# Two gated products in a seven-product block form: a decoder trunk on one Trainium2 core

## The chip, the cores and the metric

The kernel runs on one core of one Trainium2 chip, as one program. The metric is the device time of one execution in microseconds (us), the median over runs. Engines are named as in the profile: PE (TensorE matmul) and PEld (its weight load), DVE (VectorE), ACT (ScalarE), POOL (GpSimd), SP (SyncE, which issues the transfers here).

## The reference, cut to what matters

A trunk of two layers over 528 tokens (16 learned ones and 512 real ones) with 1024 channels: a state-space layer with a GLU, a feed-forward net, an attention layer, a second feed-forward net, a last norm. The feed-forward net is what the change touches:

```python
def rmsnorm(x, gain):
    x32 = x.astype(jnp.float32)
    y = x32 * lax.rsqrt(jnp.mean(x32 * x32, axis=-1, keepdims=True) + RMS_EPS)
    return (y * gain.astype(jnp.float32)).astype(x.dtype)

def swiglu_ffn(h, w_in, w_out):
    gu = jnp.einsum('bld,df->blf', h, w_in)
    g, u = jnp.split(gu, 2, axis=-1)
    return jnp.einsum('blf,fd->bld', jax.nn.silu(g) * u, w_out)

h = h + swiglu_ffn(rmsnorm(h, norm_ffn[i]), w_ffn_in[i], w_ffn_out[i])
```

D_MODEL is 1024 and D_FF 2816, all in float32. "Both gated products" are the einsum with `w_in`, gate and up, of both layers.

## The kernel before

Channels lie on the 128 partitions, tokens along the free axis: `h[k]` is k-tile k (of KD = 8) with 528 columns, 512 from the attention on. Every weight matrix is cut into tiles of 128 output channels. A matmul with float32 accuracy is made from three terms: weight and operand are each split into a high part of type fp32r and the rest, w = wh + wl and x = xh + xl, and wh xh, wh xl and wl xh are summed in PSUM.

The order of everything is written out by hand: each engine executes its instructions in the order in which the program issues them. The weights are one list, `steps`, of up to 8 k-tiles (128x1024) each. `w_load` issues their transfers on SP into three buffers, two steps ahead; `w_split` (from L102) makes wh on ACT (L113) and wl = raw - wh on DVE (L114); `w_next` splits AHEAD = 2 steps ahead and gives a step to the matmuls; `mm_steps` (from L124, matmul at L135) runs the k-tiles and the three terms over one or two column blocks.

`ffn` serves both feed-forward nets. For each of KF = 22 blocks f of hidden channels it makes the gate (`pg`) and the up product (`pu`): in layer 0 in two column blocks of 264 each, 2 x 8 x 3 x 2 = 96 matmuls, in layer 1 in one block of 512 columns (`pgu`), 48 matmuls. Then DVE scales the gate by `rstd` (L809), ACT makes Silu (L810), POOL multiplies it by `rstd` (L811), DVE multiplies by the up product (L812), ACT makes `hh` (L813) and DVE `hl` (L814). After all 22 blocks the projection out (`po`) runs over d = 0 to 7 with 22 k-tiles each in three steps (8, 8 and 6 k-tiles), adds to `h[d]` (L826, L828), and sums squares on POOL (`ssq_add`, L162 to L166). `split_x` (L156, L157) makes the xh and xl of the next stage. `tail` is the last d of layer 1 with the final norm, in two halves of 256 columns (L1180).

PSUM in `ffn` is four tiles of two banks each. The hidden tiles `hh` and `hl` of all 22 blocks lie in SBUF at once.

Of the kernel before, what the change touches and what calls it, by code (L numbers as in the profile page):

```python
# [30 lines left out]
AHEAD = 2  # L31
SQB = 6
# [11 lines left out]
OFF = {0: 0, 1: 128, 2: 256, 3: 384}  # L44


@with_exitstack
def trunk_kernel(ctx, tc, xu, xn, prm, octp, gvec, c_id, c_rev, c_i16, c_blk, c_mask,
# [19 lines left out]

    def add_w(src, n, kt):
        for f in range(n):  # L70
            k0 = 0
            while k0 < kt:
                nk = min(8, kt - k0)
                steps.append((src, f, k0, nk))
                k0 += nk

    for f in range(N1F):
        steps.append((w_glu, f, 0, GLU1[f]))
    for f in (2 * p_ + j for p_ in PAIRS for j in ((0, 1) if p_ != PAIRS[-1] else (1, 0))):
# [12 lines left out]

    def w_load(n):
        while state["load"] <= min(n, len(steps) - 1):
            i = state["load"]
            src, f, k0, nk = steps[i]
            r = raw_p.tile([128, 8, 128], F32, tag="raw", name=f"raw{i}")
            sp.dma_start(out=r[:, 0:nk, :], in_=src[f, :, k0 * 128:(k0 + nk) * 128].rearrange("p (k m) -> p k m", m=128))
            raws[i] = r
            state["load"] += 1  # L100

    def w_split(n):  # L102
        while state["split"] <= min(n, len(steps) - 1):
            i = state["split"]
            w_load(i + 2)
            src, f, k0, nk = steps[i]
            r = raws.pop(i)[:, 0:nk, :]
            if alt:
                wh, wl = alt.pop(0)()
            else:  # L110
                wh = wh_p.tile([128, 8, 128], F32R, tag="wh", name=f"wh{i}")
                wl = wl_p.tile([128, 8, 128], F32R, tag="wl", name=f"wl{i}")
            act.activation(out=wh[:, 0:nk, :], in_=r, func=ACTF.Copy)  # L113
            dve.tensor_tensor(out=wl[:, 0:nk, :], in0=r, in1=wh[:, 0:nk, :], op=ALU.subtract)  # L114
            splits[i] = (wh, wl)
            state["split"] += 1

    def w_next(ahead=AHEAD):
# [3 lines left out]
        return splits.pop(i), steps[i][3], steps[i][2]  # L122
# [35 lines left out]

    def ssq_add(k, ssq, n, first):
# [1167 lines left out]
```

## Time and profile before

| | us |
|---|---|
| median of 3 runs | 1281.71 (1281.14 to 1282.2) |
| profiled execution, its own time | 1283.81 |
| its span, first to last instruction | 1282.0 |
| PE busy | 1207.2 (94%) |
| DVE busy | 707.8 (55%) |
| ACT busy | 484.6 (38%) |
| POOL busy | 326.4 (25%) |
| gate/up products of layer 0 | about 233 to 489 |
| projection out of layer 0 | about 489 to 617 |
| gate/up products of layer 1 | about 898 to 1145 |
| projection out of layer 1 | about 1145 to 1270 |

A busy time is the sum of what the profile shows for an engine's instructions; where an instruction waits for a port inside its own run, the wait is part of it. Matmuls are pipelined, so what one costs is read from start to start, not from its own duration. The stages are told apart by the tiles that the matmuls write (`pg`, `pu`, `pgu`, `po`).

### The profile page before, as it was taken

How to read it: one execution, taken by the hardware profiler on the slowest of the kernel's cores; microseconds unless marked ns; L12 is line 12 of the kernel's file. 1: busy time of each engine (PE TensorE's matmuls, PEld its weight loads, DVE VectorE, ACT ScalarE, POOL GpSimd, SP SyncE). 2: the span in 40 equal slices, each digit the busy share in tenths (PEclk: the TensorE clock that was granted, in tenths of full speed). 3: DMA queues.
4: the chain of work that ended last, by engine and by line, in shares of the span. 5: the costliest groups of instructions: out<-in, count | busy, mean ns of one | idle time of the engine just before them, and what ended most of it. 6: DMA issues, size and time to landing. Idle time of an engine off the chain costs nothing.

```text
span 1282.0 us, 19763 instructions
## 1 busy us (share of the span) xinstructions
PE 1207.2 (94%) x8206; PEld 1100.9 (86%) x8206; DVE 707.8 (55%) x987; ACT 484.6 (38%) x738; POOL 326.4 (25%) x290
## 2 busy tenths in 40 slices
PE   3588899999999999999989999989999999999996
PEld 3578899999999999999979999868788888888886
DVE  8899547643433343433678888985644444442224
ACT  5544343432223222222557666753332323321120
POOL 6444027210110110111144444444311101111110
PEclk8689899999999999999999999999999999999998
DMA  3455523232233323333212221122233333223321
GB/s 98 88 110 114 106 77 110 77 117 86 83 100 86 94 81 91 91 91 95 87 50 57 62 64 50 50 66 80 69 99 99 99 99 94 88 88 96 102 74 66
DMA packets 44919, 110.15 MB, mean 86 GB/s; under 512 B 4766, under 2 KB 17950, under 8 KB 44830
## 3 DMA queue, kind: packets, MB, share of 16 engines
q1 hardware_dynamic: 43024, 107.64, 29.5%
q8 instruction: 64, 1.05, 0.3%
q10 hardware_dynamic: 1805, 1.26, 0.3%
q14 instruction: 26, 0.20, 0.1%
HBM read 106.14 MB, written 2.74 MB: 85 GB/s over the span
## 4 chain that ended last, share of the span: by engine, by line
PE 73%; DVE 6%; ACT 1%; issue 1%; POOL 0%; DVEq 0%; ACTq 0%; POOLq 0%
PE pgu L135 19%; PE po L135 18%; PE pu L135 10%; PE pg L135 10%; PE pj L135 7%; PE pj L1089 2%; DVE ga L985 2%; PE w L1027 1%; PE pv L1048 1%; PE po L1180 1%; DVE wl L114 1%; PE z L977 1%; PE z L1089 1%; PE z L976 1%; DVE xl L157 1%
## 5 line engine op out<-in xcount | busy, mean ns | idle before, releaser
L114 DVE TENSOR_TENSOR wl<-raw,wh 128x1024 fp32r<-128x1024 f32 (+5 forms) x194 | 242.8, 1257 | 223.8 <-ACT wh L113 220.4
L113 ACT ACTIVATE wh<-raw 128x1024 fp32r<-128x1024 f32 (+5 forms) x194 | 189.1, 979 | 242.4 <-PE po L135 120.2
L811 POOL TENSOR_TENSOR s<-s,rstd 128x528 f32<-128x528 f32 (+1 forms) x44 | 57.4, 1305 | 439.7 <-ACT s L810 439.7
L135 PE MATMUL pgu<-xl,wh 128*128 128x512 f32 x352 | 138.7, 394 | 1.0 <-DVE xl L157 1.0
L135 PE MATMUL pgu<-xh,wh 128*128 128x512 f32 x352 | 138.3, 393 | 0.6 <-ACT xh L156 0.6
L135 PE MATMUL pgu<-xh,wl 128*128 128x512 f32 x352 | 138.4, 393 | 0.0
L135 PE MATMUL po<-hh,wh 128*128 128x264 f32 (+1 forms) x506 | 132.0, 317 | 0.0
L135 PE MATMUL po<-hh,wl 128*128 128x264 f32 (+1 forms) x506 | 131.9, 317 | 0.0
L135 PE MATMUL po<-hl,wh 128*128 128x264 f32 (+1 forms) x506 | 131.8, 317 | 0.0
L135 PE MATMUL pg<-xh,wl 128*128 128x264 f32 x536 | 109.5, 286 | 2.3 <-DVE wl L114 2.3
L135 PE MATMUL pg<-xl,wh 128*128 128x264 f32 x536 | 109.6, 286 | 1.9 <-DVE xl L157 1.9
L135 PE MATMUL pg<-xh,wh 128*128 128x264 f32 x536 | 110.2, 287 | 1.2 <-ACT ysb L627 0.9
L998 POOL TENSOR_TENSOR be<-be,ga 128x415 f32<-128x415 f32 (+1 forms) x48 | 58.1, 1210 | 127.5 <-DVE ga L985 111.5
L135 PEld LDWEIGHTS po<-hh,wh 128*128 128x128 f32 x506 | 83.2, 188 | 7.2
L135 PEld LDWEIGHTS po<-hl,wh 128*128 128x128 f32 x506 | 83.3, 187 | 7.1
L135 PEld LDWEIGHTS po<-hh,wl 128*128 128x128 f32 x506 | 83.1, 188 | 7.1
L810 ACT ACTIVATE s<-g 128x528 f32<-128x528 f32 (+1 forms) x44 | 28.1, 638 | 153.9 <-DVE g L809 153.9
L135 PEld LDWEIGHTS pg<-xh,wl 128*128 128x128 f32 x536 | 83.3, 189 | 2.7 <-DVE wl L114 2.7
L135 PEld LDWEIGHTS pg<-xh,wh 128*128 128x128 f32 x536 | 83.5, 188 | 2.4 <-ACT ysb L627 1.6
L135 PEld LDWEIGHTS pg<-xl,wh 128*128 128x128 f32 x536 | 83.1, 188 | 2.6 <-DVE xl L157 2.6
L165 POOL TENSOR_TENSOR sq<-h 128x528 f32<-128x528 f32 (+1 forms) x27 | 36.8, 1363 | 173.2 <-DVE h L826 94.1
L135 PEld LDWEIGHTS pgu<-xl,wh 128*128 128x128 f32 x352 | 66.0, 188 | 17.0 <-DVE xl L157 1.7
(338 smaller groups left out, 2566.8 us busy)
## 6 DMA issues: line engine op xcount, KB each, us to landing
raw<-in_w_in SPq DMA_DIRECT2D x88, 512.0 KB, 3.5
raw<-in_w_out SPq DMA_DIRECT2D x32, 512.0 KB, 3.8
raw<-in_w_kv SPq DMA_DIRECT2D x16, 512.0 KB, 3.6
raw<-in_w_out SPq DMA_DIRECT2D x16, 384.0 KB, 3.2
m<-rd SPq DMA_DIRECT2D x8, 512.0 KB
raw<-in_w_q SPq DMA_DIRECT2D x8, 512.0 KB, 3.5
raw<-in_w_o SPq DMA_DIRECT2D x8, 512.0 KB, 3.4
op<-in_octp SPq DMA_DIRECT2D x8, 352.0 KB, 7.1
```

Of the source, the lines that this page charges most:

```text
L113: act.activation(out=wh[:, 0:nk, :], in_=r, func=ACTF.Copy)
L114: dve.tensor_tensor(out=wl[:, 0:nk, :], in0=r, in1=wh[:, 0:nk, :], op=ALU.subtract)
L135: pe.matmul(ps[pc][:, 0:n], lhsT=w[:, k, :], rhs=x[kk][:, c0:c0 + n], start=(first and k == 0 and j == 0), stop=(last and k == nk - 1 and ...
L157: dve.scalar_tensor_tensor(out=xl[k], in0=h[k][:, 0:n], scalar=g, in1=xh[k], op0=ALU.mult, op1=ALU.subtract)
L165: e.tensor_tensor(out=sq[:, 0:n], in0=h[k][:, 0:n], in1=h[k][:, 0:n], op=ALU.mult)
L810: act.activation(out=s_, in_=g_, func=ACTF.Silu)
L811: pool.tensor_tensor(out=s_, in0=s_, in1=rstd[:, 0:n], op=ALU.mult)
L976: pe.matmul(o_, lhsT=qhh[hd][:, q0:q0 + 128], rhs=khl[hd][:, k0:k0 + nn], start=True, stop=False)
L977: pe.matmul(o_, lhsT=ql[hd][:, q0:q0 + 128], rhs=khl[hd][:, k0:k0 + nn], start=False, stop=True)
L985: dve.tensor_tensor_scan(out=ga[:, c0:c1], data0=ga[:, c0:c1], data1=hide[:, m0:m0 + c1 - c0], initial=init, op0=ALU.mult, op1=ALU.max)
L998: pool.tensor_tensor(out=be[:, 1:n], in0=be[:, 1:n], in1=ga[:, 0:n - 1], op=ALU.mult)
L1089: pe.matmul(ps, lhsT=w[:, k, :], rhs=x[k], start=(k == 0 and j == 0), stop=(k == KD - 1 and j == 2))
```

## The change

The gate/up product of a block f becomes one 2 x 2 block product in seven multiplications in place of eight. The weights are cut into A11 (gate, k-tiles 0 to 3), A12 (gate, 4 to 7), A21 (up, 0 to 3), A22 (up, 4 to 7); the operand into B11, B12 (k-tiles 0 to 3, first and second half of the tokens), B21, B22 (k-tiles 4 to 7). Weight sums are S1 = A21 + A22, S2 = S1 - A11, S3 = A11 - A21, S4 = A12 - S2; operand sums T1 = B12 - B11, T2 = B22 - T1, T3 = B22 - B12, T4 from T2 and B21. Products are numbered P1 (A11 B11), P2 (A12 B21), P3 (S4 B22), P4 (A22 T4), P5 (S1 T1), P6 (S2 T2), P7 (S3 T3). Each is 4 k-tiles times three split terms over half the tokens (264 columns in layer 0, 256 in layer 1).

P1 and P2 share a PSUM bank, P5 and P3 another, P7 and P4 a third; the rest of the sums is made on DVE. The weight sums are made on POOL from the raw tiles, and each of the seven weight operands is split on ACT and DVE by itself. The hidden blocks run in three chunks (6, 8 and 8 blocks), each with its own projection out into `h`, so that `hh` and `hl` hold one chunk. `steps` now has two kinds of entries (d: direct, b: block); `b_next` splits up to BAHEAD = 4 products ahead, POOL's sums are issued up to five steps before that, and the raw tiles of odd blocks get buffers of their own. At the entry of each layer the seven operands are made from `h` (class `Combos`) in place of eight `split_x`; the squares of the last `h` tile go to the norm as a sum of their own. The lines that this takes from the diff, cut:

```diff
+BAHEAD = 4
+CHUNKS = ((0, 6), (6, 14), (14, 22))
+WHICH = {1: "A11", 2: "A12", 3: "S4", 4: "A22", 5: "S1", 6: "S2", 7: "S3"}
+XOF = {1: "B11", 2: "B21", 3: "B22", 4: "T4", 5: "T1", 6: "T2", 7: "T3"}
+def products(f0, f1):
+    out = []
+    for f in range(f0, f1):
+        if f == 0:
+            out += [(1, 0), (1, 1), (5, 0), (5, 1)]
+        elif f > 1:
+            out += [(1, f), (5, f)]
+        if f > f0:
+            out += [(3, f - 1), (4, f - 1)]
+        out += [(6, f), (2, f), (7, f)]
+    return out + [(3, f1 - 1), (4, f1 - 1)]
...
+    def make_sum(L, f, tag):
...
+        pool.tensor_tensor(out=t, in0=a, in1=b, op=op)
...
+    def sums_ahead(i, to):
+        for j in range(max(0, i - 4), min(i + to, len(steps) - 1) + 1):
+            if steps[j][0] == "b" and steps[j][2] == 5 and f"u{(steps[j][1], steps[j][3])}" in raws and steps[j][1] in scope:
+                all_sums(steps[j][1], steps[j][3])
...
+                _, L, m, f = steps[i]
+                loads_to(i, 11)
+                sums_ahead(i, 5)
+                r = block(L, m, f)
...
+                act.activation(out=wh, in_=r, func=ACTF.Copy)
+                dve.tensor_tensor(out=wl, in0=r, in1=wh, op=ALU.subtract)
...
+            def mm(p, ps, first, last):
+                wh, wl = b_next()
+                for k in range(4):
+                    xh, xl = cx.c[XOF[p], k]
+                    for j, (w, x) in enumerate(((wh, xh), (wh, xl), (wl, xh))):
+                        pe.matmul(ps[:, 0:m], lhsT=w[:, k], rhs=x, start=(first and k == 0 and j == 0),
+                                  stop=(k == 3 and j == 2), skip_group_check=True)
...
+            for c, (f0, f1) in enumerate(CHUNKS):
+                for q, (p, f) in enumerate(products(f0, f1)):
...
+                    mm(p, s[tag], p in (1, 5, 6, 7), True)
...
+                    if p == 1:
+                        s["m1"] = half_tile("m1")
+                        act.activation(out=s["m1"], in_=ps, func=ACTF.Copy)
+                    elif p == 6:
...
+                        add(s["u1"], ps, s["m1"])
+                        add(s["uu"][:, m:n], s["Z"][:, 0:m], s["u1"])
...
+                    elif p == 2:
+                        s["g"] = ft.tile([128, n], F32, tag="g", name="g")
+                        dve.tensor_tensor(out=s["g"][:, 0:m], in0=ps, in1=rstd[:, 0:m], op=ALU.mult)
+                    elif p == 7:
+                        add(s["uu"][:, m:n], ps, s["uu"][:, m:n])
+                    elif p == 3:
+                        g_ = s["g"]
+                        add(g_[:, m:n], ps, s["u1"])
+                        dve.tensor_tensor(out=g_[:, m:n], in0=g_[:, m:n], in1=rstd[:, m:n], op=ALU.mult)
+                        s["s"] = ft.tile([128, n], F32, tag="s", name="s")
+                        act.activation(out=s["s"], in_=g_, func=ACTF.Silu)
+                        pool.tensor_tensor(out=s["s"], in0=s["s"], in1=rstd[:, 0:n], op=ALU.mult)
+                    elif p == 4:
+                        add(s["uu"][:, 0:m], ps, s["u1"])
...
+                        dve.tensor_tensor(out=s["s"], in0=s["s"], in1=s["uu"], op=ALU.mult)
+                        act.activation(out=hh[i], in_=s["s"], func=ACTF.Copy)
+                        dve.tensor_tensor(out=hl[i], in0=s["s"], in1=hh[i], op=ALU.subtract)
...
+                for d in range(KD):
...
+                    for _ in mm_steps(ps, Off(hh, f0), Off(hl, f0), cols):
+                        pass
+                    for pc, c0, nn in cols:
+                        dve.tensor_tensor(out=h[d][:, c0:c0 + nn], in0=h[d][:, c0:c0 + nn], in1=ps[pc][:, 0:nn], op=ALU.add)
```

## Rows read from the trace of the kernel before

**Rows 1.** The page, part 1: busy us (share of the span), instructions

```profile
PE 1207.2 (94%) x8206; PEld 1100.9 (86%) x8206; DVE 707.8 (55%) x987; ACT 484.6 (38%) x738; POOL 326.4 (25%) x290
```

**Rows 2.** Busy time by stretch (gate/up of layer 0, of layer 1), columns named

```profile
core 0: us, PE busy (x) PEld busy (x) DVE busy (x) ACT busy (x) POOL busy (x), PEclk, DMA share, GB/s
255.00:488.00 233.00, 233.00 (x1906) 233.00 (x1905) 90.23 (x102) 66.61 (x81) 27.44 (x21) 1.00 0.32 94
...
913.00:1145.00 232.00, 232.00 (x1005) 188.32 (x1005) 97.64 (x111) 71.09 (x87) 27.03 (x21) 1.00 0.30 94
```

**Rows 3.** The chain that ended last, in order: start us, us, what

```profile
254.35 5.87 PE pg L135 x48
260.23 5.87 PE pu L135 x48
...
912.53 232.98 PE pgu L135 x1008
```

**Rows 4.** Timeline of PE in the tail, 256 columns: start us, us, instruction

```profile
1253.14 0.28 PE L1180 MATMUL po<-hh,wh 128*128 128x256 f32 x1
...
1257.91 0.28 PE L1180 MATMUL po<-hh,wh 128*128 128x256 f32 x1
```

**Rows 5.** Timeline of POOL, ACT and DVE, one block; an addition of 512 columns

```profile
346.06 1.32 POOL L811 TENSOR_TENSOR s<-s,rstd 128x528 f32<-128x528 f32 x1 [10.42 <-ACT s L810]
...
345.27 0.65 ACT L810 ACTIVATE s<-g 128x528 f32<-128x528 f32 x1 [1.91 <-DVE g L809]
...
349.85 0.71 DVE L814 TENSOR_TENSOR hl<-s,hh 128x528 fp32r<-128x528 f32 x1 [0.71 <-ACT hh L813]
...
1178.92 1.28 POOL L166 TENSOR_TENSOR ssq<-ssq,sq 128x512 f32<-128x512 f32 x1
```

**Rows 6.** Timeline of DVE: a split of 512 columns, two PSUM operations of 264

```profile
193.27 0.68 DVE L114 TENSOR_TENSOR wl<-raw,wh 128x512 fp32r<-128x512 f32 x1
...
706.00 0.43 DVE L876 TENSOR_TENSOR kf<-pj,rstd 128x264 f32<-128x264 f32 x1
706.35 0.42 DVE L877 TENSOR_TENSOR kf<-pj,rstd 128x264 f32<-128x264 f32 x1
```

**Rows 7.** Timeline at the entry of layer 1: DVE's splits, then POOL's squares

```profile
896.15 1.77 DVE L157 SCALAR_TENSOR_TENSOR xl<-h,gv,xh 128x512 fp32r<-128x512 f32 x1
...
897.84 1.52 DVE L157 SCALAR_TENSOR_TENSOR xl<-h,gv,xh 128x512 fp32r<-128x512 f32 x1
...
895.73 1.64 POOL L166 TENSOR_TENSOR ssq<-ssq,sq 128x512 f32<-128x512 f32 x1
897.45 1.37 POOL L165 TENSOR_TENSOR sq<-h 128x512 f32<-128x512 f32 x1
898.90 1.61 POOL L166 TENSOR_TENSOR ssq<-ssq,sq 128x512 f32<-128x512 f32 x1
```

**Rows 8.** Timeline of DVE and POOL in the projection out of layer 0

```profile
525.37 0.94 DVE L114 TENSOR_TENSOR wl<-raw,wh 128x768 fp32r<-128x768 f32 x1
...
539.70 2.08 DVE L114 TENSOR_TENSOR wl<-raw,wh 128x768 fp32r<-128x768 f32 x1
...
539.29 1.67 POOL L166 TENSOR_TENSOR ssq<-ssq,sq 128x528 f32<-128x528 f32 x1
```

**Rows 9.** Timeline of the GLU: DVE operations that read PSUM, POOL beside them

```profile
217.63 0.69 DVE L760 TENSOR_TENSOR part<-part,pg 128x528 f32<-128x528 f32 x1
218.25 0.69 DVE L762 TENSOR_TENSOR part<-part,pv 128x528 f32<-128x528 f32 x1
...
216.71 2.19 POOL L166 TENSOR_TENSOR ssq<-ssq,sq 128x528 f32<-128x528 f32 x1
```

**Rows 10.** Timeline of ACT: a weight copy of 512 columns

```profile
191.65 0.62 ACT L113 ACTIVATE wh<-raw 128x512 fp32r<-128x512 f32 x1
```

**Rows 11.** Busy time by stretch around a fall of the clock, columns as in group 2

```profile
638.00:654.00 16.00, 11.77 (x70) 10.01 (x68) 13.72 (x16) 9.59 (x16) 7.57 (x6) 1.00 0.30 96
654.30:657.50 3.20, 2.97 (x11) 2.52 (x12) 0.69 (x1) 0.82 (x2) 1.87 (x3) 0.50 0.02 5
```

More of the change, by code (lines that the diff above doesn't have):

```diff
@@ L87, in trunk_kernel @@
     add_w(w_o, KD, KD)
-    add_w(w_in1, 2 * KF, KD)
-    add_w(w_out1, KD, KF)
+    add_ffn(1, w_in1, w_out1)
     raws, splits, alt = {}, {}, []
     state = {"load": 0, "split": 0, "use": 0}
-    def w_load(n):
[L94 to L100, printed above, removed]
+    scope, sums, half = {}, {}, []
@@ new lines, in all_sums, with block @@
+    def all_sums(L, f):
+        for tag in ("S1", "S2", "S3", "S4"):
+            if (L, f, tag) not in sums:
+                make_sum(L, f, tag)
+    def block(L, m, f):
+        g, u = raws.get(f"g{(L, f)}"), raws.get(f"u{(L, f)}")
+        which = WHICH[m]
+        if which in ("A11", "A12"):
+            return None if g is None else g[:, 0:4] if which == "A11" else g[:, 4:8]
+        if which == "A22":
+            return None if u is None else u[:, 4:8]
+        return sums.get((L, f, which))
@@ L121, in w_next, with b_next @@
         state["use"] += 1
-        return splits.pop(i), steps[i][3], steps[i][2]
+        return splits.pop(i), steps[i][4], steps[i][3]
+    tile_no, opened = [], False
+    for st in steps:
+        tile_no.append(tile_no[-1] + (not opened) if tile_no else 0)
+        opened = st[0] == "b" and not opened
+    def b_next(ahead=BAHEAD):
+        i = state["use"]
+        n = min(i + ahead, len(steps) - 1)
+        while tile_no[n] > tile_no[i] + 2:
+            n -= 1
+        w_split(n)
+        state["use"] += 1
+        return splits.pop(i)
     def mm_steps(ps, xh, xl, cols, first=True, last=True, split_at=0, by_bank=False):
@@ L778, in ffn @@
+        sq7 = rs_p.tile([128, NTOK], F32, tag="sq", name="sq7")
+        act.activation(out=sq7, in_=h[KD - 1], func=ACTF.Square)
+        w_split(step_of[0, 5, 0])
+        cx.main()
+        for j in range(4):
+            cx.split("T1", j)
+        cx.second(3, cx.t["s", 3][:, 1], cx.t["s", 3][:, 2])
+        for name in ("T2", "T3"):
+            for j in range(4):
+                cx.split(name, j)
+    def ffn(L, cx, n, cols, ssq, before, gain_out, ssq_out, xo, extra=None, tail=None):
         m = n // 2
@@ new lines, in late @@
+            def late(q):
+                if q in (1, 2):
+                    for j in (2 * q - 2, 2 * q - 1):
+                        cx.split("B22", j)
+                elif q in (3, 4):
+                    for j in (2 * q - 6, 2 * q - 5):
+                        cx.fourth(j, hp_.tile([128, n], F32, tag=f"hh{j}", name="t4"))
+            st_, rstd = {}, None
+            hh, hl = {}, {}
+            def mm(p, ps, first, last):
[5 more added lines that the diff above has]
+                                  stop=(k == 3 and j == 2), skip_group_check=True)
@@ new lines, in trunk_kernel, with once, get, b21 @@
+    lazy = {}
+    def once(name, make):
+        def get():
+            if name not in lazy:
+                lazy[name] = make()
+            return lazy[name]
+        return get
+    def b21(cx):
+        def go():
+            for j in range(4):
+                cx.split("B21", j)
+        return go
+    xkv, xq = once("kv", lambda: x_tiles(NTOK)), once("q", lambda: x_tiles(NREAL, 0, 2, "s"))
+    get2 = once("ssq2", lambda: new_ssq(NTOK))
+    ffn(0, cx, NTOK, COLS_A, [ssq, sq7], b21(cx), G_KV, get2, xkv, lambda d: split_x(d, xq()[0], xq()[1], NREAL, G_MIX1) if d < 2 else None)
@@ L1225, in tail @@
         add_sq(0)
-        half(1, {8: (h1,), 20: (h2,)})
+        half(1, {3: (h1,), 7: (h2,)})
         add_sq(1)
```

349 lines of the change are left out of this document (241 added, 108 removed).

## The prediction

> **What bounds the kernel now.** I read the engines' shares first, then the busy time by stage, then the chain that ended last. TensorE is busy 94% of the span [rows 1]; in the two gate/up stages it is busy without a break, at full granted clock, while VectorE works 90.2 of 233 us and 97.6 of 232 us, and GpSimd some 27 us in either [rows 2]. The chain agrees: in layer 0 one gate or up tile after the other, 5.87 us per 48 matmuls of 264 columns (122.3 ns each); in layer 1 1008 matmuls of 512 columns in 232.98 us (231.1 ns each) [rows 3]. So both stages are TensorE's, and a hidden block f costs 2 x 5.87 = 11.74 us in layer 0 and 48 x 0.2311 = 11.09 us in layer 1: 258.3 and 244.0 us for 22 blocks.
>
> **What the change takes from TensorE.** Seven products of 4 k-tiles x 3 terms are 84 matmuls a block, where 96 half-width ones (layer 0) or 48 full ones (layer 1) stood. Layer 0: 84 x 0.1223 = 10.27 us. Layer 1 has 256 columns now; the tail of before runs that shape, 42 starts in 4.77 us, 113.6 ns each [rows 4], so 84 x 0.1136 = 9.54 us. The gain at most is 22 x 1.47 + 22 x 1.55 = 66.4 us. The projection out keeps its matmuls; it drains PSUM three times as often, on a VectorE that has little else to do there, which I count at nothing (if that cover were gone: 16 further drains a layer of 0.7 us, 22 us in all).
>
> **What it adds to the other engines, a block.** VectorE: seven splits of 512 columns (0.68 us as shown, 0.60 from start to start, on the line between the 264- and the 528-column rows); six sums or scalings of half width with one operand in PSUM (0.42, 0.35 start to start); one scaling in SBUF (0.35); s x uu and hl as before (0.70, start to start 0.62) [rows 5, 6, 9]. That is 4.2 + 2.1 + 0.35 + 1.24 = 7.9 us of issue. ScalarE: seven copies of 0.62 [rows 10], one of PSUM, Silu and hh at 0.65 [rows 5]: some 6 us, no bound. GpSimd: four sums of 512 columns at 1.28 and s x rstd at 1.32 [rows 5]: 6.5 us. By busy time alone all fits beside TensorE's 10.27 us.
>
> **Why it doesn't fit.** GpSimd and VectorE are not independent here. A split of 768 columns takes 0.94 us alone and 2.08 us where a GpSimd addition runs [rows 8]. At the entry of layer 1 both engines alternate: each two-operand addition on GpSimd (1.28 alone) takes 1.61 to 1.64 us, each VectorE operation that meets it 1.77; the next VectorE operation starts 1.69 us after, and VectorE ends 0.55 us after the addition, the next addition 1.15 us after VectorE [rows 5, 7]. So an addition and a VectorE operation of 512 columns cost 0.55 + 1.15 = 1.70 us as a pair, where side by side they would cost the addition's 1.36 (1.28 and a gap of 0.08). An operation with an operand in PSUM is spared: 0.69 us beside an addition that itself ran 2.19 [rows 9]. Of the 16 VectorE operations of a block ten have both operands in SBUF (seven splits, the scaling, s x uu, hl), and all five of GpSimd's read SBUF. The least that ten and five can take is 5 x 1.70 + 5 x 0.58 = 11.4 us, over 10.27 already.
>
> The Trainium skill (SBUF — State Buffer, section "SBUF: two separate sides") speaks against this change: VectorE with two SBUF inputs and GpSimd take a shared port pair in turn, each for the whole instruction, the loser waiting. By it a pair would be the plain sum, 0.60 + 1.36 = 1.96 us, where rows 7 show 1.70; I use the row.
>
> **The queues, walked once.** VectorE takes its work in program order, so a wait holds all behind it. Read from the diff, the order of one block is: wl(P1), uu, s x uu, hl, wl(P5), u1, uu, wl(P3), g, wl(P4), uu, wl(P6), wl(P2), wl(P7), g, scaling. GpSimd's is s x rstd, S1, S2, S3, S4 (four sums for two blocks ahead, S4 after wl(P3) since its tile comes free there). With zero at the end of the scaling: Silu until 0.68, and the copy for wl(P1) behind it on ScalarE until 1.22; s x rstd until 2.14; wl(P1), which met it, until 2.69; uu; s x uu waits for S1 (3.84) until 4.41; hh, then hl, which waits for S2 (5.56), until 6.13; wl(P5) waits for S3 (7.28) until 7.83; two PSUM operations; wl(P3) until 9.12; S4 9.2 to 10.5; wl(P4), which met it, until 11.05; the six left end at 13.85. Of that 2.0 us are waits for ScalarE and 4.5 us waits for GpSimd. Where the raw tiles of an odd block land later, the sums slide back and it is 13.6; I take 13.7 in layer 0, 13.6 in layer 1. The splits of a block are then up to four products ahead of TensorE, its 10.27 us fit inside, and it idles about 3.4 us a block: VectorE's line sets the pace. Without sums in the block the same walk gives 10.6 and 10.4 us.
>
> How many blocks have the sums: they are issued some eight products ahead, so that those of 6 of a layer's 22 blocks (the first two of each chunk) fall into the entry or the projection out, where VectorE has time. Layer 0: 16 x 13.7 + 6 x 10.6 = 282.8, 24.5 more than 258.3. Layer 1: 16 x 13.6 + 6 x 10.4 = 280.0, 36.0 more than 244.0.
>
> **Entries and chunk ends.** Each layer's entry now makes seven operands of half width: some 48 VectorE operations (B11, B21, B22, T1 to T4 and their splits) for 8 of 528 columns. About 14 hide under the last GLU or o product; 34 x 0.35 = 12 us are left, and seven GpSimd sums beside them, while four products (5.9 us) can already run. Bounds: nothing, and 20 us where each meets a sum; I take 10 us a layer, since the products of k-halves 0 to 3 need none of the late ones. At a chunk's end the last block's chain (scaling to hl, 4.2 us without sums) must end before the projection reaches its last k (3.7 to 5.1 us into it), and the last PSUM product is 1.5 us behind: 0 to 3 us each, I take 1.5, six times: 9 us. No transfer is added.
>
> **Sum.** The profiled execution took 1283.8 us (span 1282.0), 2.1 over the median of 1281.7. 1283.8 + 24.5 + 36.0 + 20 + 9 = 1373.3; against the median 1371. Bounds of the period: 11.4 us in the sixteen blocks and TensorE's pace in the six gives 244.0 and 239.6 us, which with 8 us for entries and ends is 1273, 1271 by the median; 14.5 us, with 40 and 18 us for them, is 1430 and 1427.
>
> **Rivals.** One: TensorE stays the bound, since the sums slip into times in which VectorE waits or reads PSUM (2.1 us of PSUM operations and 2.0 us of waits a block speak for it). Then 1283.8 - 66.4 + 10 = 1227, 1225 by the median. It decides from a period of about 10.8 us, at which 32 such blocks with the rest equal the time before; the least of 11.4 by rows 7 speaks against. Two: the ports alternate as I say, but the queues settle into a better packing, 11.4 to 12.8 us: 1271 to 1344, mostly slower. Three: the plain sum of the skill's rule above. As a mechanism of this kernel each of five pairs a block costs 1.96 for 1.70, the period goes to 15.0, and the time to 1371 + 32 x 1.35 = 1414. Four: the clock. In before the granted clock fell to 0.50 in the 3 us after a stretch in which TensorE was busy 11.8 of 16 us [rows 11]; I put it at 10.27 of 13.7 here. One such fall per block costs 1.6 us of matmul time, which the 3.4 us of idle time would take; if the clock stayed at half, a block's 84 matmuls would take 20.5 us and the 32 blocks add over 200 us. Five: that the change doesn't do fewer matmuls: by its loops it does, so no chance is set aside.
>
> **How the numbers follow.** Forecast (period 13.0 to 14.4): 0.60, 1348 to 1400. TensorE bound: 0.11, faster. Better packing: 0.18, of which 0.04 faster, 0.04 even, 0.10 slower. Plain sum: 0.06. Clock at half for long: 0.05, over 1430. The range of 1271 to 1425 leaves out the TensorE-bound case and the long fall of the clock. A measurement of this kernel can tell about 0.2% (2.6 us) from no change. Faster 0.15, within 0.2% 0.04, slower 0.81.
>
> **What would show it.** Right: in the gate/up stages of after VectorE is busy (its blocked time counted) above 90%, TensorE some 75%; splits of 512 columns have a median well over 0.68 us, up to 1.8; GpSimd's sums take 1.6; TensorE's longest wait is for wl or wh; a block spans 13 to 14 us where sums run and under 11 where none do; the chain runs through VectorE and GpSimd. Wrong: splits at 0.6 to 0.7 us beside sums, the chain on TensorE with 10.3 us a block, or the time lost at entries and chunk ends and not in the blocks.

## The result and the profile after

The changed kernel takes 1420.66 us (median of 4 runs, 1419.13 to 1423.03) where the kernel before takes 1281.95 in the same comparison: a ratio of 1.108 (95% interval 1.105 to 1.110), 139 us slower. The forecast was slower, 1371 us, 89 us over before. So direction and range held, and some 50 us of the loss were not foreseen. The profiled execution of after took 1420.7 us (span 1418.8), so its rows stand for the median.

The page first: part 1 (busy time, share of the span, instructions), the granted clock in 40 slices from part 2, and the chain that ended last by engine from part 4.

```profile
PE 1212.9 (85%) x8700; PEld 1130.8 (80%) x8700; DVE 1059.9 (75%) x1607; ACT 588.5 (41%) x1052; POOL 581.6 (41%) x462
...
PEclk7799998799999999999999999997799999999998
...
PE 45%; DVE 36%; ACT 9%; issue 6%; POOL 2%; DMA 2%; DVEq 0%; ACTq 0%; POOLq 0%; SPq 0%
```

Against [rows 1], TensorE's share falls from 94 to 85%, and VectorE's busy time rises by 352 us, GpSimd's by 255. VectorE now has 36% of the chain that ended last. In before it had 6%, and in the gate/up stages TensorE had the chain without a break [rows 3]; before's line of the same part of its page:

```profile
PE 73%; DVE 6%; ACT 1%; issue 1%; POOL 0%; DVEq 0%; ACTq 0%; POOLq 0%
```

Busy time by stretch, in order: around the entry of layer 0's gated product, up to the sixth product of its second block; layer 0's second chunk of hidden blocks; the same two for layer 1; layer 1's third chunk.

```profile
core 0: us, PE busy (x) PEld busy (x) DVE busy (x) ACT busy (x) POOL busy (x), PEclk, DMA share, GB/s
217.60:272.50 54.90, 30.63 (x178) 29.20 (x177) 41.72 (x76) 25.37 (x53) 23.04 (x17) 0.75 0.19 65
370.40:477.30 106.90, 90.97 (x675) 86.87 (x674) 89.84 (x127) 41.67 (x77) 46.80 (x32) 0.95 0.23 75
955.20:1008.30 53.10, 26.55 (x133) 24.38 (x132) 40.96 (x70) 20.22 (x43) 25.84 (x20) 0.69 0.17 60
1104.40:1210.20 105.80, 90.13 (x673) 86.54 (x672) 88.10 (x126) 41.46 (x77) 47.00 (x33) 0.92 0.24 77
1255.40:1359.50 104.10, 84.06 (x673) 79.92 (x672) 88.39 (x126) 40.85 (x76) 45.99 (x31) 1.00 0.23 74
```

Beside [rows 2], TensorE is no longer busy without a break in any of them. The two entries stand out: TensorE is busy 56 and 50% of them, VectorE 76 and 77%.

Where the time went follows from the starts of the stages in the two traces. "Forecast" is what the prediction's terms give for the same stretch: before's own time for it, plus the term.

| stretch, us | before | after | more | forecast more |
|---|---|---|---|---|
| up to the first gate/up product | 227.1 | 229.4 | 2.3 | in the entry |
| layer 0, gate/up and projections out | 390.0 | 447.5 | 57.5 | 24.5 + 10 + 4.5 |
| from there to the first product of layer 1 | 280.7 | 290.1 | 9.4 | in the entry |
| layer 1, gate/up to the end | 384.0 | 451.8 | 67.8 | 36.0 + 10 + 4.5 |

Cut by chunk, the first of each layer is the one that is off. It took 105.9 us in layer 0 where the terms give 91.2 (four blocks of 13.7, two of 10.6, 1.5 for the end, 10 for the entry, and the 3.7 that before's 262.0 us stood above 22 x 11.74); in layer 1 it took 103.6 for 90.1 by the same count. The second and third took 106.8 and 105.2 for 104.9, and 105.8 and 104.1 for 103.9. The projections out took 129.6 us in layer 0 (before 128.0) and 126.2 in layer 1 (124.3).

So of the 47 us that the span is over the forecast, 2.3 + 9.4 + 14.7 + 13.5 = 40 lie at the two entries. With the 10 us foreseen for each, an entry costs 27 us in layer 0 and 33 in layer 1: 60 of the 137 us by which the span grew.

**A block with sums.** VectorE in layer 0's second chunk, from the scaling that ends one block to the one that ends the next (start us, us, line, operation, then the idle time before it and its releaser):

```profile
412.45 0.43 DVE L1067 TENSOR_TENSOR g<-g,rstd 128x264 f32<-128x264 f32 x1
414.11 1.39 DVE L233 TENSOR_TENSOR wl<-raw,wh 128x512 fp32r<-128x512 f32 x1 [1.23 <-ACT wh L232]
415.43 0.42 DVE L1035 TENSOR_TENSOR uu<-W,u 128x264 f32<-128x264 f32 x1
415.95 0.71 DVE L1076 TENSOR_TENSOR s<-s,uu 128x528 f32<-128x528 f32 x1
417.37 1.00 DVE L1078 TENSOR_TENSOR hl<-s,hh 128x528 fp32r<-128x528 f32 x1 [0.71 <-ACT hh L1077]
418.30 1.75 DVE L233 TENSOR_TENSOR wl<-S,wh 128x512 fp32r<-128x512 f32 x1
...
420.78 0.96 DVE L233 TENSOR_TENSOR wl<-S,wh 128x512 fp32r<-128x512 f32 x1
...
422.00 1.72 DVE L233 TENSOR_TENSOR wl<-rawu,wh 128x512 fp32r<-128x512 f32 x1
...
423.99 0.68 DVE L233 TENSOR_TENSOR wl<-S,wh 128x512 fp32r<-128x512 f32 x1
...
426.25 0.43 DVE L1067 TENSOR_TENSOR g<-g,rstd 128x264 f32<-128x264 f32 x1
```

GpSimd in the same block, columns alike:

```profile
413.64 1.32 POOL L1070 TENSOR_TENSOR s<-s,rstd 128x528 f32<-128x528 f32 x1 [4.26 <-ACT s L1069]
416.44 1.37 POOL L181 TENSOR_TENSOR S<-rawu 128x512 f32<-128x512 f32 x1 [1.48 <-DMA rawu<-in_w_in]
417.88 1.62 POOL L181 TENSOR_TENSOR S<-S,rawg 128x512 f32<-128x512 f32 x1
419.47 1.73 POOL L181 TENSOR_TENSOR S<-rawg,rawu 128x512 f32<-128x512 f32 x1
421.88 1.29 POOL L181 TENSOR_TENSOR S<-rawg,S 128x512 f32<-128x512 f32 x1 [0.69 <-DVE wl L233]
```

The block lasts 13.80 us, the shortest of its chunk: from scaling to scaling VectorE's blocks with sums take 13.8 to 14.6 us in layer 0 (mean 14.1) and 13.7 to 14.0 in layer 1 (13.9), and the last two of a chunk, without sums, 11.1 and 10.4 to 10.7, 11.0 and 9.7 to 10.5. Two splits of the same size, at 422.00 and 423.99, take 1.72 and 0.68: the first meets GpSimd's S4 (421.88 to 423.17), the second meets nothing. All VectorE operations that are long here (at 414.11, 417.37, 418.30, 420.78, 422.00) lie beside one of GpSimd's five. Against the lengths that they have alone (0.68, 0.71 for hl) they lose 0.71, 0.29, 1.07, 0.28 and 1.04 us, 3.4 together. Outside them VectorE has no gap but the 1.23 and 0.71 us for ScalarE. With nothing on GpSimd a block of VectorE's takes 10.3 us in layer 0 (the run "TensorE's pace" below), so the five meetings are nearly all of the difference.

### The profile page after: what moved, and what is told of

It is laid out like the page before. It is cut to its first block, busy times and chain, and to the rows that moved or that the text cites. A ratio compares the mean times of both kernels' runs of the same rounds, so it can differ in the third digit from the quotient of the medians.

```text
span 1418.8 us, 22103 instructions
## 1 busy us (share of the span) xinstructions
PE 1212.9 (85%) x8700; PEld 1130.8 (80%) x8700; DVE 1059.9 (75%) x1607; ACT 588.5 (41%) x1052; POOL 581.6 (41%) x462
## 4 chain that ended last, share of the span: by engine, by line
PE 45%; DVE 36%; ACT 9%; issue 6%; POOL 2%; DMA 2%; DVEq 0%; ACTq 0%; POOLq 0%; SPq 0%
DVE wl L233 15%; PE X L269 7%; PE Z L269 6%; PE pj L269 6%; PE pg L269 4%; ACT wh L232 3%; PE Z L1028 3%; PE W L1028 3%; DVE s L1076 2%; PE Y L269 2%; PE W L269 2%; DVE uu L1035 2%; DVE hl L1078 2%; DVE wl L216 1%; ACT hh L1077 1%
## 5 line engine op out<-in xcount | busy, mean ns | idle before, releaser
L233 DVE TENSOR_TENSOR wl<-S,wh 128x512 fp32r<-128x512 f32 x176 | 167.9, 955 | 24.2 <-ACT wh L232 24.2
L216 DVE TENSOR_TENSOR wl<-raw,wh 128x1024 fp32r<-128x1024 f32 (+6 forms) x106 | 136.8, 1297 | 37.1 <-ACT wh L215 36.4
L1070 POOL TENSOR_TENSOR s<-s,rstd 128x528 f32<-128x528 f32 (+1 forms) x44 | 57.5, 1307 | 235.4 <-ACT s L1069 235.4
L215 ACT ACTIVATE wh<-raw 128x1024 fp32r<-128x1024 f32 (+6 forms) x106 | 96.0, 916 | 105.5 <-PE Z L269 24.9
L232 ACT ACTIVATE wh<-S 128x512 fp32r<-128x512 f32 x176 | 105.3, 618 | 64.5 <-POOL S L181 31.6
L1028 PE MATMUL Z<-B,wh 128*128 128x264 f32 (+1 forms) x352 | 74.5, 309 | 30.9 <-DVE uu L1035 24.1
L1028 PE MATMUL W<-T,wh 128*128 128x264 f32 (+1 forms) x352 | 72.5, 305 | 27.4 <-DVE uu L1035 27.3
L233 DVE TENSOR_TENSOR wl<-raw,wh 128x512 fp32r<-128x512 f32 x70 | 79.6, 1138 | 20.3 <-ACT wh L232 19.6
L1028 PEld LDWEIGHTS Z<-B,wh 128*128 128x128 f32 x352 | 62.2, 216 | 32.3 <-ACT wh L215 18.1
L269 PE MATMUL pj<-xh,wh 128*128 128x264 f32 (+1 forms) x256 | 62.1, 314 | 3.2 <-DVE vf L1153 2.3
L269 PE MATMUL X<-hh,wh 128*128 128x264 f32 (+1 forms) x176 | 60.5, 344 | 0.0
## 6 DMA issues: line engine op xcount, KB each, us to landing
raw<-in_w_out SPq DMA_DIRECT2D x16, 384.0 KB
```

The source lines that it names most:

```text
L232: act.activation(out=wh, in_=r, func=ACTF.Copy)
L233: dve.tensor_tensor(out=wl, in0=r, in1=wh, op=ALU.subtract)
L269: pe.matmul(ps[pc][:, 0:n], lhsT=w[:, k, :], rhs=x[kk][:, c0:c0 + n], start=(first and k == 0 and j == 0), stop=(last and k == nk - 1 and ...
L1028: pe.matmul(ps[:, 0:m], lhsT=w[:, k], rhs=x, start=(first and k == 0 and j == 0), stop=(k == 3 and j == 2), skip_group_check=True)
L1070: pool.tensor_tensor(out=s["s"], in0=s["s"], in1=rstd[:, 0:n], op=ALU.mult)
```

## The experiments

Every run is compared with the kernel before. The theory: the blocks are slow because GpSimd's additions read SBUF and hold up VectorE's operations with two SBUF operands; what follows on the entries came out of the first runs. Rivals: the plain amount of VectorE's work, TensorE's own pace, the chunks, and the order of the work at the entry.

| run | us | ratio to before (95%) |
|---|---|---|
| sums left out | 1329.21 | 1.036 (1.034 to 1.038) |
| sums on VectorE | 1382.54 | 1.078 (1.076 to 1.079) |
| GpSimd writes, reads nothing | 1331.77 | 1.039 (1.036 to 1.041) |
| each sum twice | 1561.76 | 1.217 (1.215 to 1.220) |
| before, in three chunks | 1286.81 | 1.004 (1.002 to 1.005) |
| no sums, no s x rstd | 1296.93 | 1.011 (1.009 to 1.013) |
| other order at the entry | 1427.95 | 1.114 (1.112 to 1.116) |
| that, and sums on VectorE | 1384.45 | 1.080 (1.079 to 1.082) |
| first two blocks without sums | 1410.73 | 1.099 (1.098 to 1.101) |
| one operand | 1384.64 | 1.079 (1.076 to 1.082) |
| T4 not made | 1411.80 | 1.100 (1.098 to 1.102) |
| no sums, no s x rstd, one operand | 1250.41 | 0.974 (0.973 to 0.976) |

**Do the sums set the pace of a block?** In `make_sum`, ahead of the addition:

```diff
+        sums[L, f, tag] = {"S1": a21, "S2": a11, "S3": a21, "S4": a22}[tag]
+        return
```

> The changed kernel with GpSimd's four weight sums left out: the splits of S1 to S4 read a raw weight block instead (A21, A11, A21, A22), all else the same. Port theory (GpSimd's additions hold up VectorE's splits): blocks fall from 13.4 to 14.3 us to the 10.2 to 10.6 us that the first block of a chunk shows, 32 blocks x 3.3 = 105 us less, and some 15 us less at the two entries: 1290 to 1315 us. Rival (VectorE's own longer queue sets the pace): splits keep their length, 1390 to 1420 us.

It took 1329.21 us, 91 under after and 14 over the range expected. By VectorE's scalings the blocks went from 14.1 to 11.1 us in layer 0 and from 13.9 to 11.0 in layer 1; 62 of the 91 us lie in the four later chunks, 27 in the first ones. What was not expected is how much the first chunks keep: 92.8 and 90.2 us, where six blocks of 11.1 and 11.0 are 67 and 66. There the question of the entries began.

**Is it the work, or who does it?** The same additions on VectorE, which gives the engine that sets the pace four more operations a block:

```diff
-        pool.tensor_tensor(out=t, in0=a, in1=b, op=op)
+        dve.tensor_tensor(out=t, in0=a, in1=b, op=op)
...
-                sums_ahead(i, 5)
+                sums_ahead(i, 1)
```

> The changed kernel with the four sums on VectorE instead of GpSimd, issued four products later so that VectorE doesn't wait for a transfer. VectorE then has 4 x 0.60 = 2.4 us more work a block. Port theory: a sum on GpSimd costs VectorE more in waiting (about 0.8 us each) than the sum itself, so the kernel gets faster: blocks at 12.9 to 13.2 us, 32 x 0.7 = 22 us less, and some 10 us less at the entries: 1380 to 1400 us. Rival (VectorE's amount of work is the bound, GpSimd runs beside it): 2.4 x 32 = 77 us more, 1490 us or above.

As expected: 1382.54 us, 38 faster than after, with blocks of 12.7 and 12.6 us. The sums' tile in the trace of this kernel (count: shortest/median/longest ns):

```profile
L181 DVE TENSOR_TENSOR S<-S,raw x24: 691/692/697, 236.4 to 1285.3; 128x512 f32<-128x512 f32 x24
...
L181 DVE TENSOR_TENSOR S<-raw,raw x22: 684/1784/1812, 237.0 to 1285.9; 128x512 f32<-128x512 f32 x22
```

A sum costs VectorE 0.69 us. The third of a block's four costs 1.78, since it alone meets what GpSimd still does, s x rstd. Against the blocks without sums (11.1 and 11.0) the four add 1.6 us, 0.4 each, since they also fill the 1.23 us in which VectorE waited for ScalarE. An amount of work that made the kernel faster when it was added speaks against the plain amount as the cause.

**Is it GpSimd's reading?** Two writes of a constant stand in place of each addition, so that GpSimd still writes and hands over every tile, in twice as many instructions, but reads nothing:

```diff
-        pool.tensor_tensor(out=t, in0=a, in1=b, op=op)
+        pool.memset(t, 0.01)
+        pool.memset(t, 0.02)
```

> The changed kernel with each weight sum on GpSimd replaced by two fills of the same tile with a constant: GpSimd still writes the tile that the split waits for, but reads no SBUF (the sums are left out). If GpSimd's reading is what holds VectorE up, blocks come down to the 11.0 us of the run without sums: 1315 to 1345 us. If any GpSimd instruction on SBUF does, or if waiting for GpSimd's result does, the blocks stay at 13 us and above: 1390 us or more.

1331.77 us, within 3 us of the run with no sums at all, and blocks of 11.1 and 11.0 as there. The tile of the sums in this kernel (shortest/median/longest ns), GpSimd's writes and VectorE's splits, and then VectorE and GpSimd in two blocks:

```profile
L181 POOL MEMSET S<- x176: 517/526/542, 223.6 to 1243.9; 128x512 f32 x176
L234 DVE TENSOR_TENSOR wl<-S,wh x176: 678/682/1392, 232.6 to 1259.9; 128x512 fp32r<-128x512 f32 x176
...
415.94 1.40 DVE L234 TENSOR_TENSOR wl<-raw,wh 128x512 fp32r<-128x512 f32 x1 [1.23 <-ACT wh L233]
...
411.06 0.68 DVE L234 TENSOR_TENSOR wl<-raw,wh 128x512 fp32r<-128x512 f32 x1
...
415.46 1.32 POOL L1071 TENSOR_TENSOR s<-s,rstd 128x528 f32<-128x528 f32 x1 [3.48 <-ACT s L1070]
...
410.86 0.53 POOL L181 MEMSET S<- 128x512 f32 x1 [2.04 <-DVE wl L234]
```

The split at 411.06 has a write of GpSimd beside it and takes 0.68 us; the one at 415.94 has s x rstd beside it, which still reads, and takes 1.40. Of the 308 splits of this form 40 take over 0.8 us here, 38 of them 0.47 us behind the start of an s x rstd, as many as in the run without sums; in after it is 135. The median hides this, since under half are long in either kernel. The lines of after for the sums' tile (the additions of S3 stand for GpSimd's):

```profile
L233 DVE TENSOR_TENSOR wl<-S,wh x176: 674/684/1793, 232.0 to 1350.9; 128x512 fp32r<-128x512 f32 x176
...
L181 POOL TENSOR_TENSOR S<-raw,raw x22: 1257/1750/1774, 238.7 to 1316.3; 128x512 f32<-128x512 f32 x22
```

GpSimd is busy 1.05 us a sum here against 1.3 to 1.75, so it is not quite the same load; but a loss that went with GpSimd's load would not have gone whole with a third less of it. The Trainium skill ("SBUF — State Buffer", section "SBUF: two separate sides") says that an operation of VectorE with two SBUF inputs contends only with one of GpSimd that reads SBUF. This run agrees.

**The dose the other way.** Each sum twice:

```diff
         pool.tensor_tensor(out=t, in0=a, in1=b, op=op)
+        pool.tensor_tensor(out=t, in0=a, in1=b, op=op)
```

> The changed kernel with each of GpSimd's sums made twice into the same tile (the second writes the same values). Port theory: four more additions a block, each costing VectorE's line 0.9 to 1.1 us: blocks at 17.4 to 18.2 us, 32 x 4 = 125 us more and some 18 us at the entries: 1550 to 1575 us. Rival (GpSimd has idle time, 15.6 of 36 us in the blocks, and only its latency counts): under 1450 us.

1561.76 us, in the range, and blocks of 17.0 us, a little under the expected 17.4 to 18.2 (the first full block of each later chunk took 19.3 to 23.0). Four more additions cost 2.9 us a block in layer 0 and 3.1 in layer 1, 0.7 to 0.8 each where 0.9 to 1.1 was expected. The median of the splits of S went up:

```profile
L234 DVE TENSOR_TENSOR wl<-S,wh x176: 680/1432/1800, 235.8 to 1492.7; 128x512 fp32r<-128x512 f32 x176
```

**The chunks alone.** The kernel before, its steps and its projections out in three chunks:

```diff
...
+        for f0, f1 in CHUNKS:
+            for f in range(2 * f0, 2 * f1):
+                steps.append((w_in, f, 0, KD))
+            for d in range(KD):
+                steps.append((w_out, d, f0, f1 - f0))
...
```

> The kernel before with only one part of the change: the hidden blocks in three chunks (6, 8, 8), each with its projection out, products as before. The prediction counted the further drains of PSUM at nothing and a chunk's end at 1.5 us: 1282 to 1292 us. Rival (the chunks cost a good part of the loss, by drains and restarts): 1310 us or above.

1286.81 us: the chunks cost 4 us (3 to 6) and are not where the time went.

**TensorE's pace.** Sums left out as above, and GpSimd's last operation of a block with them:

```diff
-                        pool.tensor_tensor(out=s["s"], in0=s["s"], in1=rstd[:, 0:n], op=ALU.mult)
```

> The changed kernel without the four sums (raw blocks in their place) and without the multiplication by rstd on GpSimd before the up product, so that GpSimd does nothing in the blocks; both are left out. Without sums the blocks took 11.0 us. Port theory: the last contention (s x rstd against one split) and its latency go, and TensorE becomes the bound, 10.2 us in layer 0 and 9.7 in layer 1: some 36 blocks x 1.0 less than without sums, 1285 to 1300 us. Rival (VectorE's own 7.9 us and its waits for ScalarE set 11 us): 1320 to 1330 us.

1296.93 us. TensorE's blocks take 10.15 us in layer 0 and 9.8 to 10.3 in layer 1, where 10.27 and 9.54 were worked out for 84 matmuls. Two of VectorE's scalings in layer 1:

```profile
1078.06 0.43 DVE L1070 TENSOR_TENSOR g<-g,rstd 128x256 f32<-128x256 f32 x1
...
1088.27 0.43 DVE L1070 TENSOR_TENSOR g<-g,rstd 128x256 f32<-128x256 f32 x1
```

VectorE's own line takes 10.33 us a block in layer 0 and 10.22 in layer 1, with no wait but the two for ScalarE. So with GpSimd gone the two engines are close: in layer 0 TensorE keeps its pace over a chunk, while in layer 1 it runs at 9.79 as long as the splits in store last and at VectorE's 10.2 in the last three blocks. The dose is nearly straight: with no, one, five and nine GpSimd operations a block lasts 10.3, 11.1, 14.1 and 17.0 us in layer 0 and 10.2, 11.0, 13.9 and 17.0 in layer 1, 0.7 to 0.8 us for each. Still the kernel is not under the time before: its first chunks take 86.8 and 87.1 us, where six blocks at TensorE's pace would take 61 and 59 to 62.

**The entry: order.** In after, TensorE stands still long three times in layer 0's entry, and once ahead of layer 1's, whose entry has three more of 5.6 to 6.7 us (matmuls with a long wait, PE's timeline):

```profile
243.12 0.59 PE L1028 MATMUL Z<-T1h,wh 128*128 128x264 f32 x1 [6.66 <-ACT wh L232]
...
261.00 0.78 PE L1028 MATMUL Z<-B,wh 128*128 128x264 f32 x2 [7.17 <-DVE uu L1035]
...
269.73 0.78 PE L1028 MATMUL W<-T,wh 128*128 128x264 f32 x2 [5.75 <-DVE uu L1035]
...
967.02 0.55 PE L1028 MATMUL X<-B11h,wh 128*128 128x256 f32 x1 [8.06 <-DVE h L1429]
```

The first waits for S1 of the second block (rawu in GpSimd's row), whose sum runs fourth in a row that begins late: its first sum waited until T3 was split on VectorE. The raw tile itself comes late too: its transfer goes out only then, which is SP's line below.

```profile
237.02 0.33 SPq L162 DMA_DIRECT2D rawu<-in_w_in  x1
...
237.17 1.58 POOL L181 TENSOR_TENSOR S<-S,raw 128x512 f32<-128x512 f32 x1 [6.47 <-DVE T3l L299]
...
241.15 1.26 POOL L181 TENSOR_TENSOR S<-rawu 128x512 f32<-128x512 f32 x1
```

Most of this wait is the transfer's and not the sum's. In the run "TensorE's pace", which has no sums, the transfer goes out at 237.31, the same matmul still waits 5.94 us, and ScalarE ahead of it waits for the transfer:

```profile
240.96 0.63 ACT L235 ACTIVATE wh<-rawu 128x512 fp32r<-128x512 f32 x1 [4.47 <-DMA rawu<-in_w_in]
```

The second waits until a read of block 0's bank Z is through, which stands on VectorE behind the making of T4; the third for a read of bank W, which stands behind the rstd chain. VectorE at that place:

```profile
252.01 0.48 DVE L325 SCALAR_TENSOR_TENSOR t<-h,gv,T2h 128x264 f32<-128x264 f32 x1
...
259.61 0.43 DVE L299 TENSOR_TENSOR T<-t,T 128x264 fp32r<-128x264 f32 x1 [0.49 <-ACT T L298]
...
260.42 0.43 DVE L1035 TENSOR_TENSOR uu<-Z,u 128x264 f32<-128x264 f32 x1
...
262.92 1.86 DVE L390 TENSOR_TENSOR s<-rstd 128x528 f32<-128x528 f32 x1 [1.39 <-ACT rstd L387]
264.81 1.68 DVE L391 TENSOR_TENSOR s<-s,g 128x528 f32<-128x528 f32 x1
...
269.16 0.43 DVE L1035 TENSOR_TENSOR uu<-W,uu 128x264 f32<-128x264 f32 x1
```

So the theory for the entry was a matter of order: put those reads ahead of T4 and of the rstd chain.

```diff
-                elif q in (3, 4):
-                    for j in (2 * q - 6, 2 * q - 5):
+                elif q in (4, 5):
+                    for j in (2 * q - 8, 2 * q - 7):
...
+                    elif p == 7 and rstd is None:
+                        add(s["uu"][:, m:n], ps, s["uu"][:, m:n])
...
+                    if c == 0:
+                        late(q)
```

> The changed kernel with another order on VectorE at the two entries: the reads of the first block's PSUM banks (u1, uu of P6, uu of P7) come ahead of the T4 operands and of the rstd chain, on which TensorE's P3 and P4 wait now for 7 and 6 us. If the entry's loss is VectorE's program order ahead of these reads, each entry gets 6 to 10 us shorter: 1400 to 1409 us. If it is the amount of work at the entry (48 operations, eight sums), nothing is won: 1416 to 1424 us.

The theory failed: 1427.95 us, 7 slower than after and above both cases. The 7.17 us at Z were gone, and the wait at W became the longer one:

```profile
266.80 0.78 PE L1028 MATMUL W<-T,wh 128*128 128x264 f32 x2 [10.80 <-DVE uu L1035]
```

T4, made later, now stood ahead of that read and met the sums of the third block: its last split ends at 265.5 where it ended at 260.0. The order only chose which product waits.

**Order, with GpSimd out of it.** The same edit with the sums on VectorE.

> Sums on VectorE and the new order at the entries together. If both act by themselves the gains add up: 1382 less 12 to 20 us, 1360 to 1372 us, still 6% above the kernel before, since VectorE's line stays at 12.6 to 12.8 us a block.

A miss too: 1384.45 us, where the sums on VectorE alone gave 1382.54. The order theory was dropped; what was left was the work of the entry itself.

**Which work at the entry?** First the sums of the first two blocks left out (the edit of the first run under `if f < 2`).

> The changed kernel with the weight sums of the first two blocks of each layer left out (raw blocks in their place); all other blocks keep theirs. These eight sums stand in one row on GpSimd at the entry, and TensorE waits 6.7 us for the fourth. Compared with the run without any sums, whose sixth product of block 1 came 7.5 us (layer 0) and 5.7 us (layer 1) earlier after the entry's start, this gives 13 us less: 1403 to 1412 us. If the entry is limited by the operands alone: 1416 to 1424 us.

1410.73 us, 10 under after, in the range: 5 us a layer are the entry's sums. The first wait shrank from 6.66 to 4.4 us and is the transfer's. Then T4 not made, the fourth product reading B21.

```diff
+XOF[4] = "B21"
...
         def fourth(self, j, t):
+            return
```

> The changed kernel without the making of T4 (its product reads B21 instead, so T4 is left out): 12 of the entry's VectorE operations, which with their waits for ScalarE take 8 us of VectorE's line ahead of the reads of PSUM that TensorE waits for. By the reading that VectorE's amount of work sets the entry: 7 to 9 us less per layer, 1402 to 1408 us. If something else is as late (the rstd chain, the sums of block 2): 1412 to 1424 us.

1411.80 us, 9 under after and between the two cases, at the edge of the second (1412): the wait at Z went away, and the one at W grew to 8.7 us, behind the rstd chain. Then all operands but B11.

```diff
-                    xh, xl = cx.c[XOF[p], k]
+                    xh, xl = cx.c["B11", k]
...
         def split(self, name, j):
+            if name != "B11":
+                return
...
```

`first`, `second` and `fourth`, which make the sums of operands, return at once as well.

> The changed kernel with only B11 made at the entries; all seven products read it (B21, B22 and T1 to T4 are left out), weights and sums as in the change. If the 40 or so VectorE operations that make the other operands are what costs about 30 us a layer at the entry, and some of the 9 us ahead of layer 1, 35 to 50 us go: 1370 to 1386 us. If sums and the rstd chain limit the entry: 1400 us or more.

1384.64 us, 36 under after. Nearly all of it is at the entries: the first chunks took 91.4 and 92.4 us (after 105.9 and 103.6) and the stretch ahead of layer 1's first product 282.9 (290.1), while the later chunks took 105.0 to 107.2 as in after.

**Both causes at once.** If the blocks' loss is GpSimd's and the entries' is the operands', taking both away should leave TensorE alone. The edits of the last run and of "TensorE's pace" together.

> Left out: the weight sums (the products read raw blocks), the multiplication of s by rstd, and all operands but B11, which every product reads. Blocks at TensorE's pace as without GpSimd (10.1 us in layer 0, 9.8 to 10.3 in layer 1). If the two losses are separate, the block's in the sums and the entry's in the operands, the savings add: 1297 less the 36 us that the one operand gave is 1261 us, under the time before. If the entries without GpSimd are short of VectorE's time for the operands alone, some 50 to 60 us of entry go and it is 1235 to 1250. If what is left of the entries is something else (the splits of the weights, the rstd chain), it stays at 1275 to 1297.

1250.41 us, 2.6% under before (2.4 to 2.7%), at the upper end of the second case and 11 us under the plain sum of the first. The table of the two causes, in us:

| | seven operands | only B11 |
|---|---|---|
| sums and s x rstd on GpSimd | 1420.66 | 1384.64 |
| neither | 1296.93 | 1250.41 |

Layer 0's first two chunks in the kernel with neither, busy time by stretch, columns as above, and then its first chunk with the seven operands, still without sums and s x rstd:

```profile
227.70:295.40 67.70, 64.04 (x513) 63.30 (x514) 52.19 (x99) 35.72 (x64) 1.25 (x1) 1.00 0.26 85
330.30:414.60 84.30, 82.67 (x675) 82.31 (x674) 66.74 (x127) 41.81 (x76) 0.00 (x0) 1.00 0.29 92
```

```profile
229.80:316.60 86.80, 70.12 (x512) 68.73 (x513) 65.62 (x133) 44.61 (x87) 1.27 (x1) 0.90 0.23 73
```

The first chunk falls from 86.8 to 67.7 us, and TensorE is busy 64.0 of it. So the operands cost 46.5 us without GpSimd, 23 a layer; with the sums there, 36. The sums and s x rstd cost 124 us with the operands (the first column) and 134 without. Taken away together they give back 170 us, one at a time 36 + 124 = 160: the two causes add but for 10 us. In layer 0's entry the kernel without GpSimd still has waits of 5.9, 5.4 and 3.6 us where after has 6.7, 7.2 and 5.8; with B11 alone one of 2.2 is left.

## Why the prediction was right, and where it was wrong

**What bound the kernel before: right; TensorE's gain: right in layer 0, too large in layer 1.** Without GpSimd a block of layer 0 takes TensorE 10.15 us, and 10.27 with B11 alone, as worked out. In layer 1 it takes 9.8 to 10.3 where 9.54 was worked out from the tail of before, and no run reached that. In the kernel without either cause the three chunks take 236 us in layer 0 (before 262) and 235 in layer 1 (247), so of the at most 66.4 us 38 are seen there.

**The block: right, in size and by its mechanism.** Forecast 13.7 and 13.6 us with sums; from scaling to scaling they take 14.1 and 13.9. (Read from TensorE's products, six blocks of the second chunk took 82.7 and 80.2 us, 13.8 and 13.4 each, but one of the six took 12.2 and one 10.9.) The queue walk answers to the rows: it had 2.0 us of waits for ScalarE (1.23 + 0.71 here), a split of 0.68 that becomes 1.7 where it meets an addition [rows 7], and PSUM operations that stay at 0.42 [rows 6, 9]. Of the waits for GpSimd it had more than there are: s x uu did not wait for S1 here, since S1 came after it in time, held up by a transfer; the splits met the sums instead. The five meetings cost 3.4 us together, under the walk's 4.5 (its own steps add to some 4.1), and VectorE's line without them takes 10.2 to 10.3, over the 7.9 + 2.0 of the walk: two small misses that nearly cancel. Blocks without sums were put at 10.6 and 10.4; with s x rstd alone they take VectorE 11.1 and 11.0; TensorE passes the first of a chunk, with splits in store, in 10.2 and 9.8.

**The entries: wrong, by size.** This is the step that failed: "I take 10 us a layer, since the products of k-halves 0 to 3 need none of the late ones", with bounds of 0 and 20. They cost 27 and 33 us, over the upper bound, and the three long waits of layer 0 make 19.6 us of it. Three things were left out of it:

- The 12 us of operands were counted as VectorE's time alone. But the reads that free PSUM stand in the same row: P3 and P4 of block 0 waited 7.2 and 5.75 us for a bank, as the rows under "The entry: order" show, and not for their operands.
- Of the "four products" that "can already run" only three could. The fourth, P5 of the second block, waited 6.7 us for its weights. The prediction adds no transfer, but this one goes out late: at 236 to 241 us in the kernels that make T1 to T3, at 219 and 220 in the two with B11 alone. GpSimd's row, which begins late too, adds little to that (5.9 us without any sums).
- Of the operations that "hide under the last GLU or o product" some delay what stands ahead: layer 1's first product comes 8.06 us after the last matmul before it (0.9 with B11 alone, 0.6 in before), and with B11 alone that stretch is 7.2 us shorter.

The first two were in the diff and could have been walked as the block was; the prediction walked the queues once for a block in the middle and not for the first.

**The total: inside the range in part by luck.** 1420.66 us lies above the 1348 to 1400 that had a chance of 0.60 (by the terms given, 14.4 us a block ends at 1395). It is under 1425 because that bound had room for blocks of 14.5 us, which they didn't need; the entries, at 60 us, took more than their 40.

**Chunk ends and drains: right as far as the runs tell.** Drains were counted at nothing, 1.5 us at six ends. The projections out took 1.6 and 1.9 us more than before, and before in chunks took 4 us more in all. What a chunk's end costs by itself no run separates.

**The rivals.** TensorE as the bound (1225) is false in after; it comes near to being true when both causes are gone, at 1250. The break-even of 10.8 us a block was worked out with entries of 10 us: without GpSimd the blocks are under it at 9.8 to 10.3, and that kernel is still 1.1% slower than before, because the entries alone eat the gain. Better packing is false. The plain sum of each pair gave 1414 us, near the 1420.66; that is chance, since its period of 15.0 us is not there (14.1 and 13.9) and the rest lies in the entries. A split that begins 0.12 us into an addition of 1.29 (422.00 and 421.88 above) ends 0.55 us behind it, so it loses 1.04 us; one that begins 0.48 into s x rstd loses 0.72. By the Trainium skill's rule (the section named above) the loser waits for the whole instruction. The rows agree but for some 0.1 us, since the split alone takes 0.68; the plain sum fails because most of the five meetings begin in the middle of an instruction. The clock at half for long is false: it was granted at 0.92 to 1.00 in the blocks, and layer 1's third chunk at 1.00 took 104.1 us, its second at 0.92 took 105.8. In the entries it was 0.75 and 0.69; how much of their time is that, the runs don't tell apart.

**What would show it: half right.** The block length (13.7 to 14.6), GpSimd's 1.6 to 1.75, and the waits for wl and wh came out as said. Of the signs of being wrong one came half true: 60 of 137 us lie at the entries. The chain runs through VectorE (36%), but hardly through GpSimd (2%), whose cost is inside VectorE's instructions. VectorE was to be over 90% busy; it is 84%. The prediction's own walk has 2.0 us of waits in 13.7, which makes 85%, so this sign did not follow from the working. TensorE was to be 75%; the profile shows 85%, though 84 matmuls that take 10.15 us unhindered are 72% of 14.1. The busy share is no measure of a pace here; the block length is. And the median split was to be well over 0.68 us; it is 0.685 over all 308, with a mean of 1.04: 135 of them are over 0.8 us, under half, so the median sits among those that meet nothing. The mean, or the count of those that do, is what should have been named.

**What stays open.** No run gives the second block's raw tile and the first sums other buffers, which would show what their late start costs by itself; which of the operands' tiles the transfer waits for is not in the record. The entry is not shown to be VectorE's amount of work alone: in the 46 us from 229 us on VectorE waits 12.8 for ScalarE, 5.5 of them for the copy of that block's S1. Nor do the runs tell VectorE's part in the operands' 23 us a layer from ScalarE's, which copies their high parts. And no complete version of the block form here beats the kernel before: the best is the one with the sums on VectorE, at 1382.54 us.

## What to carry to other kernels

Before work is moved onto GpSimd beside a busy VectorE, count the pairs: a 512-column addition that reads SBUF took up to 1.1 us from the VectorE operation with two SBUF operands that met it, and 0.7 to 0.8 from a block on the mean; done by VectorE itself it added 0.4 to the block. A form with fewer products pays with operands that must be made before the pipeline runs; walk the queues of the first block as carefully as those of one in the middle, and look there for reads that free PSUM behind the making of operands, and for transfers that can only go out late. When a reordering only moves a wait to the next product, take away the work that all the waits stand behind, as the run with one operand did, before trying another order. And where a few meetings are long, count them or take the mean: a median of 0.685 us hid 135 splits of 308.

## What the runs showed of the hardware

GpSimd writing 128x512 in 0.53 us without reading left VectorE's splits of the sums at a mean of 0.71 us (6 of 176 over 0.8, where beside additions it is 60 of 176 and a mean of 0.96) and the kernel within 3 us of the one without sums. VectorE did the sums in 0.69 us each (0.6 to 0.7 from start to start) where GpSimd takes 1.3 to 1.75, and giving them to the engine that set the pace made the kernel 38 us faster. The cost of GpSimd's operations to a block was nearly straight in their number: 10.3, 11.1, 14.1 and 17.0 us with none, one, five and nine.
